# A decoder layer's down projection: all subtractions on VectorE, the operands' splits spread over five block products, two token blocks' norms without GpSimd

## The chip, the cores and the metric

One core of one Trainium2 chip runs the whole layer as one program. The metric is the device time of one execution in microseconds (us), and the time of a kernel is the median of its timed runs.

## The reference

One decoder layer on 512 tokens of width 1024, all float32: a first sublayer (sparse attention and a gated convolution, merged and projected) and a second one, the part that the change touches:

```python
gu = causal_dwconv(h @ w_ffn_up[i], ffn_conv_w[i], ffn_conv_b[i])      # 1024 -> 2 x 2816
g_ffn, u_ffn = jnp.split(gu, 2, axis=-1)
ffn = (jax.nn.silu(g_ffn) * u_ffn) @ w_ffn_down[i]                     # 2816 -> 1024
ple = jax.nn.sigmoid(h @ w_ple_gate[i] + b_ple_gate[i]) * (p[i] @ w_ple[i])
h = layer_norm(DEEPNORM_ALPHA * h + ffn + ple, ln2_g[i], ln2_b[i])     # over the 1024 columns
```

## The kernel before, in words

**Products in three parts.** Every large product is made of three matmuls. Each operand is split into a rounded copy `hi` and a rest `lo = raw - hi`, and hi·hi, hi·lo and lo·hi are summed in PSUM. A split is a copy on ScalarE (line 61 for weights, 1037 for activations; the trace calls it CAST) and then a subtraction with both inputs in SBUF. For the weights of this stage the subtraction is on VectorE (line 63), for the activations of the down projection on GpSimd (line 1038).

**Weights.** A chunk is 128x1024 (512 KB), the sixth of each product 128x512. `Chunk.dma` loads it through SP's queue into one of 4 raw buffers (`wr`), and `Chunk.split` writes `wh` and `wl`, 4 buffers each. `run` goes through a fixed list of steps. Ahead of step i, `advance` splits the chunk that step i+3 uses, and asks for the next load, which waits for the raw buffer: until VectorE has made the `wl` of four chunks before. `wh` and `wl` come free when TensorE has finished the step of four chunks before. Then the step's `preps` are issued, then the step. Engines work through their own instructions in program order.

**The down projection by seven block products.** The 2816 rows (22 groups of 128) are halved, the 1024 output columns (halves F0 and F1) too, and so are the 512 tokens: e stands for the early token blocks 0 and 1, l for the late ones 2 and 3. Seven products of half size (a Strassen scheme) take the place of eight; `PRODUCTS` names each one's weight sum, its activation operand (B11, B21, T2, T4, T3, T1, B22, in this order) and its PSUM bank. Products 0 to 5 take six steps each (11 row groups x 2 token blocks x 3 matmuls of 512 columns). The seventh (B22) takes two steps, and then one tail step for each late token block, with four chunks (38 to 41, counted from 0 at the first product). For token block 3 its columns are cut in two of 256.

**Operands.** `take_part(name, q)` splits a third of an activation operand (4, 4 and 3 groups of 128x256). Before the change the thirds of an operand are taken in steps 0, 2 and 4 of the product ahead of the one that uses it, so B22's fall into the sixth product.

**After the products.** `after_product` adds PSUM to the residual `hr` on VectorE (lines 1069, 1071) and takes statistics (1075). After the fifth product token blocks 0 and 1 are complete, and `last_norm` norms them within the sixth product (after its second and fourth step): columns F1 on VectorE by two `scalar_tensor_tensor` (lines 1139 and 1143), columns F0 by one ScalarE activation (1130) and two GpSimd operations (1131, 1132). `finish_late` adds the sixth product to blocks 2 and 3; `tail` adds the seventh, takes their last statistics and calls `last_norm` for them. Block 2 has 448 of its columns normed by GpSimd, block 3 none. Outputs of blocks 0 and 1 leave through SP's queue, in program order with the loads.

Of the kernel before, what the change touches and what calls it, by code (L numbers as in the profile page):

```python
# [8 lines left out]
F32 = mybir.dt.float32  # L9
F32R = mybir.dt.float32r  # L10
AF = mybir.ActivationFunctionType
OP = mybir.AluOpType

P = 128
S = 512
D = 1024
NB = S // P
# [20 lines left out]
class Chunk:  # L38
# [13 lines left out]
    def split(self):  # L52
        k, nc = self.k, self.k.nc
        if self.resident:
            self.hi = k.k4(f"wh{self.n}", F32R)
            self.lo = k.k4(f"wl{self.n}", F32R)
        else:
            self.hi = k.wpool.tile([P, 1024], F32R, name=f"wh{self.n}", tag="wh", bufs=k.WHL)
            self.lo = k.wpool.tile([P, 1024], F32R, name=f"wl{self.n}", tag="wl", bufs=k.WHL)
        hi, lo, raw = (t[:, self.cols] for t in (self.hi, self.lo, self.raw))  # L60
        nc.scalar.copy(hi, raw)  # L61
        eng = nc.vector if self.lo_eng == "v" else nc.gpsimd
        eng.tensor_tensor(lo, raw, hi.bitcast(F32), op=OP.subtract)  # L63


class Kern:
# [47 lines left out]

    def sm(self, name, shape, dt=F32, bufs=1):
        return self.small.tile(list(shape), dt, name=f"{name}_{self.counter()}", tag=name, bufs=bufs)

    def evac_split(self, hi, lo, src):
        self.nc.scalar.copy(hi, src)
        self.nc.vector.tensor_tensor(lo, src, hi.bitcast(F32), op=OP.subtract)  # L120
# [324 lines left out]
    def plan(self):  # L445
        nc, a = self.nc, self.a
# [5 lines left out]
        def chunk(src, **kw):  # L452
            c = Chunk(self, src, **kw)
            self.chunks.append(c)
            return c

        def step(fn, ws=()):
            i = len(self.steps)
            for w in ws:
                if w.need is None:  # L460
                    w.need = i
                w.last = i
            self.steps.append(fn)

        def wa(i, **kw):
            return chunk(a["w_a"][i], **kw)
# [286 lines left out]
        def wb(i, **kw):  # L753
            return chunk(a["w_b"][i], **kw)
# [43 lines left out]
        for i, o in enumerate(order):  # L798
            if o[0] == "g":
                w = wa(20 + 2 * o[1] + o[2], lo="p" if i <= max(att_at) else "v")  # L800
                fn = gate(o[1], o[2], w)
            elif o[0] == "r":
                w = chunk(a["w_br"][2 * o[1] + o[2]], lo="p" if i <= max(att_at) else "v")
                fn = branch(o[1], o[2], w)
            elif o[0] == "q":
                w = wa(4 + o[1], lo="v" if o[1] == 1 else "p")
                fn = qatt(o[1], w)
            else:
                w = wa(8 + 3 * o[1] + "cxb".index(o[0]), lo="p")
# [4 lines left out]
            n = att_at.get(i)  # L814
# [80 lines left out]
        for kk in range(4):  # L895
            w = wb(kk)
# [21 lines left out]
        pc, w = chunk(a["p_T"]), wb(9)  # L918
# [90 lines left out]
        for j in range(NF):  # L1009
            for which in (0, 1):  # L1010
                w = wa(36 + 2 * j + which)
                step(ffn(j, which, w), [w])
        for n, (name, i) in enumerate(copies):
# [5 lines left out]
        PRODUCTS = ((wd[0], "B11", "X"), (wd[1], "B21", "Y"), (sd["acd"], "T2", "X"), (wd[3], "T4", "W"),  # L1019
                    (sd["ac"], "T3", "X"), (sd["cd"], "T1", "Z"), (sd["abcd"], "B22", "V"))  # L1020
        self.banks, self.mv2 = {}, {}
        F0, F1 = slice(0, 512), slice(512, 1024)

        def take_part(name, q):

            n = 4 if q < 2 else HALF - 8
            if name == "B21":
                if q == 0:
                    t = [self.main.tile([P, 4, 2, S], F32R, name=f"B21{x}", tag="hT", bufs=2) for x in "hl"]
                    self.b21 = [x.rearrange("p c h (s t) -> p (c h s) t", t=256) for x in t]  # L1030
                hi, lo = (t[:, 4 * q:4 * q + 4] for t in self.b21)
            else:
                hi, lo = (self.k4(f"{name}{x}{q}", F32R, (P, 4, 256)) for x in "hl")
            for t, ts in zip((hi, lo), self.split.setdefault(name, ([], []))):
                ts.append(t)
            raw = self.part[name][q]
            nc.scalar.copy(hi[:, :n], raw[:, :n])
            nc.gpsimd.tensor_tensor(lo[:, :n], raw[:, :n], hi[:, :n].bitcast(F32), op=OP.subtract)

        def load_last():  # L1040
            self.st2 = {b: self.sm("st2", [P, 4, 6], bufs=4) for b in range(NB)}
            self.g2, self.b2 = ([self.k2(f"{n}{h}") for h in range(2)] for n in ("g2", "b2"))
            for n, ts in (("ln2_g", self.g2), ("ln2_b", self.b2)):
                v = a[n]
                for h in range(2):
                    nc.gpsimd.dma_start(ts[h], bass.AP(tensor=v.tensor, offset=v.offset + 512 * h,
                                                       ap=[[0, P], [1, 512]]))
# [18 lines left out]
        def add_to(b, fs, o, op=OP.add):  # L1066
            z = self.h1[b][:, fs]
            if op is OP.add:
                nc.vector.tensor_tensor(z, o, z, op=OP.add)  # L1069
            else:  # L1070
                nc.vector.tensor_tensor(z, z, o, op=op)

        def part_stats(b, fs):
            for i in range(fs.start // 256, fs.stop // 256):
                nc.vector.bn_stats(self.st2[b][:, i], self.h1[b][:, i * 256:i * 256 + 256])  # L1075

        def after_product(n):

            o = [x[0] for x in self.banks[PRODUCTS[n][2]]]
            for i in range(2):  # L1080
                e, l = i, 2 + i
                if n in (0, 1):
                    add_to(e, F0, o[i])
                    if n == 1:
                        part_stats(e, F0)
                elif n == 2:
                    add_to(l, F0, o[i])
                elif n == 3:
                    add_to(e, F1, o[i])
                elif n == 4:  # L1090
                    add_to(e, F1, o[i], OP.subtract)
                    part_stats(e, F1)
                    self.mv2[e] = self.ln_aggr(self.st2[e])
                    add_to(l, F1, o[i], OP.subtract)

        def finish_late(blk):

            o, b = self.banks["Z"][blk][0], 2 + blk
            add_to(b, F1, o)
            part_stats(b, F1)  # L1100
            add_to(b, F0, o, OP.subtract)

        def product(n, kk, w):
# [14 lines left out]
                    finish_late(kk)  # L1118
            return f

        def last_norm(b):
            by_pool = (512, 512, 448, 0)[b]
            z, st = self.h1[b], self.st2[b]
            rows = self.out[b * P:(b + 1) * P, :]
            gb = [[t[q.start // 512][:, q.start % 512:][:, :q.stop - q.start] for t in (self.g2, self.b2)]
                  for q in (slice(0, by_pool), F1, slice(by_pool, 512)) if q.start < 512 or q is F1]
            if by_pool:
                mv, r, nmr = self.mv2.pop(b) if b in self.mv2 else self.ln_aggr(st)
                q = slice(0, by_pool)
                nc.scalar.activation(z[:, q], z[:, q], AF.Identity, bias=nmr, scale=r)  # L1130
                nc.gpsimd.tensor_tensor(z[:, q], z[:, q], gb[0][0], op=OP.mult)
                nc.gpsimd.tensor_tensor(z[:, q], z[:, q], gb[0][1], op=OP.add)
            else:
                mv = self.sm("mv", [P, 2], bufs=4)
                nc.vector.bn_aggr(mv, st)  # L1135
                r = self.rstd(mv[:, 1:2])
            qs = list(zip([F1, slice(by_pool, 512)], gb[1:]))[:2 if by_pool < 512 else 1]
            for q, (g, _) in qs:
                nc.vector.scalar_tensor_tensor(z[:, q], z[:, q], mv[:, 0:1], g, op0=OP.subtract, op1=OP.mult)  # L1139

            def rest():
                for q, (_, be) in qs:
                    nc.vector.scalar_tensor_tensor(z[:, q], z[:, q], r, be, op0=OP.mult, op1=OP.add)  # L1143
                nc.sync.dma_start(rows[:, 512:], z[:, 512:])
                (nc.sync if b < 2 else nc.scalar).dma_start(rows[:, :512], z[:, :512])

            if b == NB - 2:
                self.pending.append(rest)
            else:
                rest()  # L1150
# [13 lines left out]
            return f  # L1164

        self.pending = []
        for n, (src, name, bank) in enumerate(PRODUCTS):
            for kk in range(NCH if n < 6 else NCH - TAILC):
                w = chunk(src[kk], cols=1024 if kk < NCH - 1 else 512)
                if n < 6 and kk % 2 == 0:  # L1170
                    nxt = PRODUCTS[n + 1][1]
                    self.preps.setdefault(len(self.steps), []).append(lambda x=nxt, q=kk // 2: take_part(x, q))
                step(product(n, kk, w), [w])
        ws = [chunk(sd["abcd"][kk], resident=kk > 3, cols=1024 if kk < NCH - 1 else 512) for kk in range(NCH - TAILC, NCH)]
        for blk in range(2):
# [2 lines left out]
        nxt = 10 ** 9  # L1178
        for c in reversed(self.chunks):
            c.due = max(min(c.need - c.lead, nxt - 1 if c.last > c.need else nxt), c.after)  # L1180
            nxt = c.due
# [124 lines left out]
```

## Time and profile before

| | us |
|---|---|
| median of 3 runs | 777.62 (777.22 to 778.82) |
| the profiled execution's own time | 781.65 |
| its span in the trace | 779.9 |
| TensorE busy, of the span | 757.8 |
| VectorE busy | 530.2 |
| ScalarE busy | 339.7 |
| GpSimd busy | 313.7 |

Times in the trace count from the span's start. The seven products run from about 659 us on. A row of the timeline gives start and duration of an instruction; on VectorE durations overlap the next instruction's start a little, so what one costs in a row of several is read from start to start. An idle time in brackets names what ended it.

### The profile page before, as it was taken

The page shows a single profiled execution, that of the slowest core. Times are in us where ns is not written, and L with a number is a line of the kernel's source. Part 1 is how long each engine was busy: PE and PEld are TensorE (multiplying, and loading weights), DVE is VectorE, ACT ScalarE, POOL GpSimd, SP SyncE. Part 2 cuts the span into 40 slices and gives each one's busy share as a digit, 9 for nine tenths or more (in the row PEclk, how much of TensorE's full clock was granted, in tenths as well). Part 3 has the DMA queues.
Part 4 walks back from the last instruction along what each step waited for, and adds up shares of the span by engine and source line. Part 5 has one row for each costly group of instructions (what it writes and reads, how often), then busy time and mean ns, then how long its engine had stood idle before and what let it go on. Part 6 is the DMA issues. An engine that isn't in the chain of part 4 may idle for free. (4 is left out here: it accounts for less than half of the span.)

```text
span 779.9 us, 9590 instructions
## 1 busy us (share of the span) xinstructions
PE 757.8 (97%) x3579; PEld 629.5 (81%) x3579; DVE 530.2 (68%) x798; ACT 339.7 (44%) x509; POOL 313.7 (40%) x230
## 2 busy tenths in 40 slices
PE   8899999999999999999999999999999999999976
PEld 5898888878878888888888888888888888888855
DVE  5878999766566349758634656566655666886797
ACT  4456334476666233242413443443343334555630
POOL 3324666643222029746211322333323332845482
PEclk9999999999999999999999999999999999999998
DMA  8372232232202156787714588777832332666551
GB/s 317 76 256 95 82 109 81 82 109 82 82 27 102 62 188 220 260 286 275 254 70 146 144 208 199 185 183 192 211 108 82 108 93 82 203 224 199 170 176 55
DMA packets 31183, 118.61 MB, mean 152 GB/s; under 512 B 3824, under 2 KB 3952, under 8 KB 30752
## 3 DMA queue, kind: packets, MB, share of 16 engines
q1 hardware_dynamic: 25536, 99.37, 36.7%
q0 software_dynamic: 4592, 16.39, 10.6%
q10 hardware_dynamic: 1008, 2.25, 0.7%
q8 instruction: 28, 0.46, 0.2%
q14 instruction: 19, 0.16, 0.1%
HBM read 112.74 MB, written 30.41 MB: 184 GB/s over the span
## 5 line engine op out<-in xcount | busy, mean ns | idle before, releaser
L63 DVE TENSOR_TENSOR wl<-wr,wh 128x1024 fp32r<-128x1024 f32 x114 | 180.9, 1604 | 104.6 <-ACT wh L61 104.6
L61 ACT CAST wh<-wr 128x1024 fp32r<-128x1024 f32 x149 | 152.1, 1027 | 77.7 <-PE dn L1064 28.1
L130 PE MATMUL ff<-h1T,wh 128*128 128x512 f32 x352 | 136.9, 389 | 0.0
L131 PE MATMUL ff<-h1T,wh 128*128 128x512 f32 x352 | 136.9, 389 | 0.0
L132 PE MATMUL ff<-h1T,wl 128*128 128x512 f32 x352 | 136.9, 389 | 0.0
L63 POOL TENSOR_TENSOR wl<-wr,wh 128x1024 fp32r<-128x1024 f32 x35 | 87.3, 2499 | 92.8 <-ACT wh L61 80.7
L130 PEld LDWEIGHTS ff<-h1T,wh 128*128 128x128 f32 x352 | 66.1, 188 | 13.8
L132 PEld LDWEIGHTS ff<-h1T,wl 128*128 128x128 f32 x352 | 66.1, 188 | 13.7
L131 PEld LDWEIGHTS ff<-h1T,wh 128*128 128x128 f32 x352 | 66.1, 188 | 13.6
L657 ACT ACTIVATE ff<-ff,vec 128x512 f32<-128x512 f32 x44 | 34.4, 781 | 79.6 <-PE ff L132 78.9
L658 DVE SCALAR_TENSOR_TENSOR ff<-ff,vec,ff 128x511 f32<-128x511 f32 x44 | 33.0, 749 | 37.1 <-ACT ff L657 37.0
L130 PE MATMUL gt<-hT,wh 128*128 128x512 f32 x128 | 50.5, 395 | 0.5 <-DVE ol L120 0.4
L132 PE MATMUL gt<-hT,wl 128*128 128x512 f32 x128 | 49.9, 390 | 0.0
L131 PE MATMUL gt<-hT,wh 128*128 128x512 f32 x128 | 49.9, 389 | 0.0
L988 POOL TENSOR_TENSOR B11l<-ff,B11h 128x256 fp32r<-128x256 f32 x11 | 8.2, 742 | 90.4 <-ACT B11h L987 90.4
L982 POOL TENSOR_TENSOR T<-T,B 128x256 f32<-128x256 f32 x11 | 9.2, 838 | 82.1 <-DVE B L978 82.1
L660 DVE SCALAR_TENSOR_TENSOR ff<-ff,vec,ff 128x510 f32<-128x510 f32 x44 | 32.9, 749 | 1.6
L130 PE MATMUL cv<-hT,wh 128*128 128x512 f32 x80 | 31.4, 392 | 0.0
L132 PE MATMUL cv<-hT,wl 128*128 128x512 f32 x80 | 31.1, 389 | 0.0
L131 PE MATMUL cv<-hT,wh 128*128 128x512 f32 x80 | 31.1, 389 | 0.0
L130 PEld LDWEIGHTS gt<-hT,wh 128*128 128x128 f32 x128 | 24.0, 188 | 6.6 <-PE lg L139 0.7
L970 ACT ACTIVATE ff<-ff 128x512 f32<-128x512 f32 x22 | 13.9, 632 | 35.0 <-DVE ff L660 35.0
(291 smaller groups left out, 1716.3 us busy)
## 6 DMA issues: line engine op xcount, KB each, us to landing
wr<-in_w_a SPq DMA_DIRECT2D x80, 512.0 KB, 3.6
wr<-in_w_b SPq DMA_DIRECT2D x17, 512.0 KB, 3.9
wr<-in_w_dn SPq DMA_DIRECT2D x15, 512.0 KB, 3.4
wr<-in_w_br SPq DMA_DIRECT2D x8, 512.0 KB, 3.3
sdac<-in_w_dn SPq DMA_DIRECT2D x6, 512.0 KB, 4.7
sdcd<-in_w_dn SPq DMA_DIRECT2D x6, 512.0 KB, 6.9
sdacd<-in_w_dn SPq DMA_DIRECT2D x6, 512.0 KB, 5.8
sdabcd<-in_w_dn SPq DMA_DIRECT2D x6, 512.0 KB, 5.5
```

The source lines that it names most:

```text
L61: nc.scalar.copy(hi, raw)
L63: eng.tensor_tensor(lo, raw, hi.bitcast(F32), op=OP.subtract)
L130: t.matmul(out, wh, xh, start=start, stop=False)
L131: t.matmul(out, wh, xl, start=False, stop=False)
L132: t.matmul(out, wl, xh, start=False, stop=stop)
L657: nc.scalar.activation(dst, src, AF.Identity, bias=v[:, bcol:bcol + 1], scale=v[:, wcol + 2 * tap:wcol + 2 * tap + 1])
L658: nc.vector.scalar_tensor_tensor(dst[:, 1:], src[:, :S - 1], v[:, wcol + tap:wcol + tap + 1], dst[:, 1:], op0=OP.mult, op1=OP.add)
L660: nc.vector.scalar_tensor_tensor(dst[:, 2:], src[:, :S - 2], v[:, wcol:wcol + 1], dst[:, 2:], op0=OP.mult, op1=OP.add)
L970: nc.scalar.activation(t, t, AF.Silu)
L982: g.tensor_tensor(p["T2"], p["T1"], second, op=OP.subtract)
L988: g.tensor_tensor(lo, first, hi.bitcast(F32), op=OP.subtract)
```

## The change

Four things change, all in the down projection.

- `take_part` puts its subtraction on VectorE. `low` is a new helper for it and for the weights' subtraction.
- The 18 thirds are no longer taken in steps 0, 2 and 4 of the product ahead, but spread over the first 30 steps (five products): number i ahead of step 8i/5. B22's last third is split ahead of step 27, not ahead of step 34. T1's split takes the two buffers that B21's has left, in place of six others.
- Token blocks 0 and 1 are normed by VectorE alone: four `scalar_tensor_tensor` each, no ScalarE activation, no GpSimd multiplication and addition. Block 2 keeps its GpSimd share.
- The statistics of blocks 0 to 2 are taken 512 columns at a time, not 256.

```diff
-        eng = nc.vector if self.lo_eng == "v" else nc.gpsimd
-        eng.tensor_tensor(lo, raw, hi.bitcast(F32), op=OP.subtract)
+        k.low(self.lo_eng, lo, raw, hi)
...
+    def low(self, eng, lo, raw, hi):
+        (self.nc.vector if eng == "v" else self.nc.gpsimd).tensor_tensor(lo, raw, hi.bitcast(F32), op=OP.subtract)
...
-            if name == "B21":
+            if name in ("B21", "T1"):
...
-            nc.gpsimd.tensor_tensor(lo[:, :n], raw[:, :n], hi[:, :n].bitcast(F32), op=OP.subtract)
+            self.low("v", lo[:, :n], raw[:, :n], hi[:, :n])
...
         def part_stats(b, fs):
-            for i in range(fs.start // 256, fs.stop // 256):
-                nc.vector.bn_stats(self.st2[b][:, i], self.h1[b][:, i * 256:i * 256 + 256])
+            w = 256 if b == NB - 1 else 512
+            for i in range(fs.start // w, fs.stop // w):
+                nc.vector.bn_stats(self.st2[b][:, i], self.h1[b][:, i * w:i * w + w])
...
-                    self.mv2[e] = self.ln_aggr(self.st2[e])
+                    self.mv2[e] = mean_rstd(self.st2[e])
...
         def last_norm(b):
-            by_pool = (512, 512, 448, 0)[b]
+            by_pool = (0, 0, 448, 0)[b]
...
-                mv = self.sm("mv", [P, 2], bufs=4)
-                nc.vector.bn_aggr(mv, st)
-                r = self.rstd(mv[:, 1:2])
-            qs = list(zip([F1, slice(by_pool, 512)], gb[1:]))[:2 if by_pool < 512 else 1]
+                mv, r = self.mv2.pop(b) if b in self.mv2 else mean_rstd(st)
+            qs = list(zip([F1, slice(by_pool, 512)], gb[1:]))
...
         self.pending = []
+        for i, (name, q) in enumerate((p[1], q) for p in PRODUCTS[1:] for q in range(3)):
+            self.preps.setdefault(len(self.steps) + 8 * i // 5, []).append(lambda x=name, q=q: take_part(x, q))
         for n, (src, name, bank) in enumerate(PRODUCTS):
             for kk in range(NCH if n < 6 else NCH - TAILC):
                 w = chunk(src[kk], cols=1024 if kk < NCH - 1 else 512)
-                if n < 6 and kk % 2 == 0:
-                    nxt = PRODUCTS[n + 1][1]
-                    self.preps.setdefault(len(self.steps), []).append(lambda x=nxt, q=kk // 2: take_part(x, q))
                 step(product(n, kk, w), [w])
```

How VectorE's instructions stand, first at the norms of token blocks 0 and 1 in the sixth product. `wl` is the rest of a weight chunk (33 to 37 here), `hr_2786` and `hr_2790` are blocks 0 and 1. Before:

```order
L63 TENSOR_TENSOR wl_6173<-wr_6074,wh_6172 128x1024
L63 TENSOR_TENSOR wl_6197<-wr_6096,wh_6196 128x1024
L1139 SCALAR_TENSOR_TENSOR hr_2786<-hr_2786,mv_6147,g_5563 128x512
L1143 SCALAR_TENSOR_TENSOR hr_2786<-hr_2786,rstd_6152,b_5565 128x512
L63 TENSOR_TENSOR wl_6222<-wr_6114,wh_6221 128x512
L63 TENSOR_TENSOR wl_6244<-wr_6136,wh_6243 128x1024
L1139 SCALAR_TENSOR_TENSOR hr_2790<-hr_2790,mv_6161,g_5563 128x512
L1143 SCALAR_TENSOR_TENSOR hr_2790<-hr_2790,rstd_6166,b_5565 128x512
L63 TENSOR_TENSOR wl_6269<-wr_6176,wh_6268 128x1024
```

Now, the same place:

```order
L118 TENSOR_TENSOR wl_6169<-wr_6084,wh_6168 128x1024
L118 TENSOR_TENSOR wl_6189<-wr_6102,wh_6188 128x1024
L1145 SCALAR_TENSOR_TENSOR hr_2786<-hr_2786,mv_6152,g_5563 128x512
L1145 SCALAR_TENSOR_TENSOR hr_2786<-hr_2786,mv_6152,g_5562 128x512
L1149 SCALAR_TENSOR_TENSOR hr_2786<-hr_2786,rstd_6156,b_5565 128x512
L1149 SCALAR_TENSOR_TENSOR hr_2786<-hr_2786,rstd_6156,b_5564 128x512
L118 TENSOR_TENSOR wl_6213<-wr_6124,wh_6212 128x512
L118 TENSOR_TENSOR wl_6231<-wr_6142,wh_6230 128x1024
L1145 SCALAR_TENSOR_TENSOR hr_2790<-hr_2790,mv_6161,g_5563 128x512
L1145 SCALAR_TENSOR_TENSOR hr_2790<-hr_2790,mv_6161,g_5562 128x512
L1149 SCALAR_TENSOR_TENSOR hr_2790<-hr_2790,rstd_6165,b_5565 128x512
L1149 SCALAR_TENSOR_TENSOR hr_2790<-hr_2790,rstd_6165,b_5564 128x512
```

Each norm is two instructions longer on VectorE, and the weights' rests behind it (chunks 35 and 36, then 37) stand behind four of them, not two.

VectorE at the start of the first product, now:

```order
L118 TENSOR_TENSOR wl_5549<-wr_5400,wh_5548 128x1024
L118 TENSOR_TENSOR B21l<-B_4771,B21h 128x1024
L118 TENSOR_TENSOR wl_5585<-wr_5436,wh_5584 128x1024
L118 TENSOR_TENSOR B21l<-B_5081,B21h 128x1024
L118 TENSOR_TENSOR wl_5605<-wr_5476,wh_5604 128x512
L118 TENSOR_TENSOR wl_5623<-wr_5512,wh_5622 128x1024
L118 TENSOR_TENSOR B21l<-B_5389,B21h 128x768
```

The operands' rests stand between the weights' rests; before the change the four `wl` stood here one behind the other, and the `B21l` on GpSimd.

GpSimd in the sixth product, before, between the two `rstd` and block 2's:

```order
L1038 TENSOR_TENSOR B22l_6179<-B_4772,B22h_6178 128x1024
L1131 TENSOR_TENSOR hr_2786<-hr_2786,g_5562 128x512
L1132 TENSOR_TENSOR hr_2786<-hr_2786,b_5564 128x512
L1038 TENSOR_TENSOR B22l_6228<-B_5082,B22h_6227 128x1024
L1131 TENSOR_TENSOR hr_2790<-hr_2790,g_5562 128x512
L1132 TENSOR_TENSOR hr_2790<-hr_2790,b_5564 128x512
L1038 TENSOR_TENSOR B22l_6275<-B_5390,B22h_6274 128x768
```

None of these seven is left on GpSimd; what it keeps there are the `rstd` of one element in each partition.

## Rows read from the trace of the kernel before

**Rows 1.** The page: busy time of each engine, its share of the span and instructions; and TensorE's granted clock in 40 slices of the span, in tenths of full speed.

```profile
PE 757.8 (97%) x3579; PEld 629.5 (81%) x3579; DVE 530.2 (68%) x798; ACT 339.7 (44%) x509; POOL 313.7 (40%) x230
PEclk9999999999999999999999999999999999999998
```

**Rows 2.** Stretches of the span: length, busy us of each engine (instructions), granted clock, DMA share, GB/s.

```profile
661.00:733.70 72.70, 72.47 (x319) 59.35 (x318) 56.68 (x44) 40.54 (x43) 43.69 (x22) 1.00 0.61 204
...
740.00:760.00 20.00, 14.43 (x64) 11.20 (x63) 19.80 (x11) 7.61 (x8) 16.67 (x8) 0.96 0.52 170
...
758.00:760.00 2.00, 2.00 (x6) 1.58 (x7) 2.00 (x2) 0.00 (x0) 0.00 (x0) 0.60 0.42 119
760.00:762.00 2.00, 2.00 (x12) 2.00 (x11) 2.00 (x4) 0.62 (x1) 0.00 (x0) 0.54 0.03 12
```

**Rows 3.** Timeline of TensorE in the down projection: start us, us, engine, line, operation, out<-in, shapes; in brackets idle time before it and what ended it.

```profile
679.10 0.50 PE L1063 MATMUL dn<-wl,B21h 128*128 128x512 f32 x1 [0.23 <-DVE wl L63]
...
718.73 0.39 PE L1062 MATMUL dn<-wh,T3h 128*128 128x512 f32 x1
...
733.69 0.39 PE L1062 MATMUL dn<-wh,T1h 128*128 128x512 f32 x1
...
748.51 0.50 PE L1063 MATMUL dn<-wl,T1h 128*128 128x512 f32 x1 [0.84 <-DVE wl L63]
...
751.84 0.50 PE L1063 MATMUL dn<-wl,B22h 128*128 128x512 f32 x1 [1.67 <-DVE wl L63]
...
757.98 0.50 PE L1063 MATMUL dn<-wl,B22h 128*128 128x512 f32 x1 [3.06 <-DVE wl L63]
...
761.85 0.28 PE L1062 MATMUL dn<-wh,B22h 128*128 128x256 f32 x1
761.97 0.28 PE L1063 MATMUL dn<-wl,B22h 128*128 128x256 f32 x1
...
766.75 0.39 PE L1064 MATMUL dn<-wh,B22l 128*128 128x512 f32 x1
```

**Rows 4.** Timeline of VectorE (DVE) from the end of the fifth product to its last rows, same columns; like neighbours are one row (x2: two instructions).

```profile
734.84 0.68 DVE L1071 TENSOR_TENSOR hr<-hr,dn 128x512 f32<-128x512 f32 x1
735.55 0.75 DVE L1075 BATCH_NORM_STATS2 st<-hr 128x6 f32<-128x256 f32 x2
736.34 0.26 DVE L168 BATCH_NORM_AGGREGATE mv<-st 128x2 f32<-128x24 f32 x1
...
739.88 2.36 DVE L63 TENSOR_TENSOR wl<-wr,wh 128x1024 fp32r<-128x1024 f32 x2
742.15 2.91 DVE L1139 SCALAR_TENSOR_TENSOR hr<-hr,mv,g 128x512 f32<-128x512 f32 x1
745.15 1.61 DVE L1143 SCALAR_TENSOR_TENSOR hr<-hr,rstd,b 128x512 f32<-128x512 f32 x1
746.69 5.10 DVE L63 TENSOR_TENSOR wl<-wr,wh 128x512 fp32r<-128x512 f32 x2
751.71 1.77 DVE L1139 SCALAR_TENSOR_TENSOR hr<-hr,mv,g 128x512 f32<-128x512 f32 x1
753.59 1.60 DVE L1143 SCALAR_TENSOR_TENSOR hr<-hr,rstd,b 128x512 f32<-128x512 f32 x1
755.11 6.83 DVE L63 TENSOR_TENSOR wl<-wr,wh 128x1024 fp32r<-128x1024 f32 x5
761.86 0.68 DVE L1069 TENSOR_TENSOR hr<-dn,hr 128x512 f32<-128x512 f32 x1
...
765.22 0.67 DVE L1071 TENSOR_TENSOR hr<-hr,dn 128x512 f32<-128x512 f32 x1
767.18 0.69 DVE L1069 TENSOR_TENSOR hr<-dn,hr 128x512 f32<-128x512 f32 x1 [1.29 <-PE dn L1064]
...
773.84 1.41 DVE L1139 SCALAR_TENSOR_TENSOR hr<-hr,mv,g 128x512 f32<-128x512 f32 x2
775.16 1.41 DVE L1143 SCALAR_TENSOR_TENSOR hr<-hr,rstd,b 128x512 f32<-128x512 f32 x2
```

**Rows 5.** Timeline of GpSimd (POOL) in the sixth product and behind it, same columns.

```profile
741.11 3.40 POOL L1038 TENSOR_TENSOR B22l<-B,B22h 128x1024 fp32r<-128x1024 f32 x1
...
747.87 2.83 POOL L1038 TENSOR_TENSOR B22l<-B,B22h 128x1024 fp32r<-128x1024 f32 x1
...
754.59 2.25 POOL L1038 TENSOR_TENSOR B22l<-B,B22h 128x768 fp32r<-128x768 f32 x1
```

**Rows 6.** Timelines of VectorE and of GpSimd in the first product and at the start of the second, same columns.

```profile
661.33 4.59 DVE L63 TENSOR_TENSOR wl<-wr,wh 128x1024 fp32r<-128x1024 f32 x3
...
670.24 5.47 DVE L63 TENSOR_TENSOR wl<-wr,wh 128x1024 fp32r<-128x1024 f32 x1 [0.97 <-ACT wh L61]
...
675.63 3.42 DVE L63 TENSOR_TENSOR wl<-wr,wh 128x1024 fp32r<-128x1024 f32 x1
...
670.39 4.22 POOL L1038 TENSOR_TENSOR B21l<-B,B21h 128x1024 fp32r<-128x1024 f32 x2
```

**Rows 7.** VectorE's line 63 from 640 us on (durations ns min/median/max); VectorE's statistics of 512 columns in the first sublayer, by line (busy us, mean ns); and the time from issue to landing of the weight loads from 640 us on.

```profile
L63 DVE TENSOR_TENSOR wl<-wr,wh x43: 677/1226/5471, 639.6 to 761.3; 128x1024 fp32r<-128x1024 f32 x36, 128x512 fp32r<-128x512 f32 x7
...
L161 DVE BATCH_NORM_STATS2 st<-hr 128x6 f32<-128x512 f32 x8 | 5.6, 695 | 0.3
...
DMA to landing us min/median/max: 2.5/3.4/6.3
```

More of the change, by code (lines that the diff above doesn't have):

```diff
@@ L1026, in take_part @@
             n = 4 if q < 2 else HALF - 8
-            if name == "B21":
+            if name in ("B21", "T1"):
                 if q == 0:
-                    t = [self.main.tile([P, 4, 2, S], F32R, name=f"B21{x}", tag="hT", bufs=2) for x in "hl"]
-                    self.b21 = [x.rearrange("p c h (s t) -> p (c h s) t", t=256) for x in t]
-                hi, lo = (t[:, 4 * q:4 * q + 4] for t in self.b21)
+                    t = [self.main.tile([P, 4, 2, S], F32R, name=f"{name}{x}", tag="hT", bufs=2) for x in "hl"]
+                    self.in_hT = [x.rearrange("p c h (s t) -> p (c h s) t", t=256) for x in t]
+                hi, lo = (t[:, 4 * q:4 * q + 4] for t in self.in_hT)
             else:
@@ L1037, in take_part @@
             nc.scalar.copy(hi[:, :n], raw[:, :n])
-            nc.gpsimd.tensor_tensor(lo[:, :n], raw[:, :n], hi[:, :n].bitcast(F32), op=OP.subtract)
+            self.low("v", lo[:, :n], raw[:, :n], hi[:, :n])
         def load_last():
-            self.st2 = {b: self.sm("st2", [P, 4, 6], bufs=4) for b in range(NB)}
+            self.st2 = {b: self.sm("st2", [P, 4, 6], bufs=4)[:, :4 if b == NB - 1 else 2] for b in range(NB)}
             self.g2, self.b2 = ([self.k2(f"{n}{h}") for h in range(2)] for n in ("g2", "b2"))
@@ L1119, in product, with mean_rstd @@
             return f
+        def mean_rstd(st):
+            mv = self.sm("mv", [P, 2], bufs=4)
+            nc.vector.bn_aggr(mv, st)
+            return mv, self.rstd(mv[:, 1:2])
         def last_norm(b):
-            by_pool = (512, 512, 448, 0)[b]
+            by_pool = (0, 0, 448, 0)[b]
             z, st = self.h1[b], self.st2[b]
@@ L1125, in last_norm @@
             gb = [[t[q.start // 512][:, q.start % 512:][:, :q.stop - q.start] for t in (self.g2, self.b2)]
-                  for q in (slice(0, by_pool), F1, slice(by_pool, 512)) if q.start < 512 or q is F1]
+                  for q in (slice(0, by_pool), F1, slice(by_pool, 512))]
             if by_pool:
-                mv, r, nmr = self.mv2.pop(b) if b in self.mv2 else self.ln_aggr(st)
+                mv, r, nmr = self.ln_aggr(st)
                 q = slice(0, by_pool)
```

## The prediction

> **What bounds the kernel now.** I read the page first, then the stretches, then the timelines of the last 45 us. The page says TensorE: 757.8 of 779.9 us busy, at a granted clock of full speed in all slices but the last [rows 1]. The stretches say the same of the first five products (72.47 of 72.70 us busy): what other engines do there costs nothing as long as TensorE isn't kept waiting. They say something else from 740 to 760: TensorE 14.43 of 20 us, VectorE 19.80, GpSimd 16.67 [rows 2]. There VectorE is what TensorE waits for. TensorE's timeline shows three stalls, of 0.84, 1.67 and 3.06 us, each ended by a `wl` of line 63; before them there is one of 0.23 us in the second product [rows 3]. [...]
>
> VectorE is full there because its instructions are long. The median `wl` takes 1.226 us, and the two at 739.88 cost 2.27 from start to start, 1.14 each; but the two at 746.69, one of them of 512 columns only, take 5.10 together. The norms' instructions take 2.91, 1.61, 1.77 and 1.60, where two of the same shape cost 1.32 and two 1.41 at the end of the kernel [rows 4, 7]. The long ones lie between 741.11 and 756.84, the start of GpSimd's first and the end of its last subtraction for B22 [rows 5]. The clearest pair is earlier: a `wl` from 670.24 takes 5.47, and GpSimd works from 670.39 for 4.22; 4.22 + 1.23 is 5.45 [rows 6]. I take from this that the long times are waits for GpSimd, which ends with GpSimd's work.
>
> **Part 1: 18 splits on VectorE, in five products.** A product takes 733.69 - 718.73 = 14.96 us of TensorE, five take 74.8 [rows 3]. VectorE's work in them: 25 `wl` of 1024 at 1.14 and 5 of 512 at 0.60 (0.677 less the same overlap of 0.08), 31.5 us [rows 4, 7]. The new ones are the same operation on the same types: 12 of 1024 at 1.14, 6 of 768 at 0.87 (halfway between), 18.9. VectorE has no such split in the trace, so the lower bound is that, the upper GpSimd's own 2.11 (4.22 for two, of 1024 and 768) [rows 6]. I take the lower, since engine, operation, size and types agree. The adds and statistics behind four products are some 3 x 1.3 + 2.8 = 6.7, eight adds and four statistics at about 0.65 and 0.75 (as the rows at 734.84 and 735.55 space them) [rows 4]. That makes 57 of 74.8 us: it fits, and TensorE covers it. A `wl` is asked for three steps (8.2 us) before its use, and the lag of before, 4.2 us at 670.24 and 2.2 at 675.63, cost TensorE 0.23 us in all [rows 3, 6]. So the splits cost nothing here, and the 0.23 goes. By the upper price VectorE would need 76 us (18 x 2.11 = 38.0 in place of 18.9), 1.4 more than there is: 770.8 in the end. ScalarE's copies only move, with 40.54 of 72.70 us used [rows 2].
>
> **Part 2: what stands behind the fifth product.** The first add starts at 734.84, now 0.23 earlier: 734.61. From it to the next `wl` it is 5.04 us now. Two pairs of statistics at 0.79 each (735.55 to 736.34) become two single ones of 0.70 + 0.04; two small instructions of one element go. I take 4.85, and `wl` 33 starts at 739.46 [rows 4, 7].
>
> **Part 3: the norms and the weights' rests.** Chunks 33 and 34 take 2.27: 741.73. Norm of block 0: four at 0.70 (1.32 and 1.41 for two), 2.80: 744.53. Chunks 35 and 36, 0.60 + 1.14: 746.27. Norm of block 1: 749.07. Chunk 37: 750.21. Chunks 38 to 40 and 41, 3.42 + 0.60: 754.23. The additions of the sixth product to blocks 2 and 3 took 761.86 to 765.89, less 0.06: VectorE is free at 758.20 [rows 4]. The price of the four is the unsure term: 0.70 alone, 1.97 as the mean of the four long ones. I take 0.70, since nothing long is left on GpSimd to meet them.
>
> [...] By the rows the path gets shorter, since the work handed out stretches what stays.
>
> TensorE then needs `wl` 35 at 747.29, 36 at 748.65, both less 0.23, 37 after a step of 6 x 0.227 + 12 x 0.12 = 2.80 more, at 751.45. They are there at 745.1, 746.3 and 750.2 (0.227 is 14.96/66, 0.12 is 761.97 - 761.85) [rows 3]. [...]
>
> **Part 4: the end.** TensorE starts the seventh product at 748.42, ends its two steps at 754.02 and block 2's 21 matmuls (4.76) at 758.78. The last of them starts at 758.56, and the add of VectorE starts 0.43 after it, as 767.18 does after 766.75: **758.99** [rows 3, 4]. VectorE has been free since 758.20, 0.79 us of slack. From here on, as before, VectorE works without a gap to the end (9.4 us) and two stores follow; that part keeps its length.
>
> **Sum.** 767.18 - 758.99 = 8.2 us. Against the profiled execution: 781.65 - 8.2 = 773.4. That one stands 4.03 us above the median of the runs; from the median it is 777.62 - 8.2 = **769.4 us**. A difference of 0.2% (1.6 us) is about what a measurement here can tell from none.
>
> **Loads.** Chunk 41's load waits for `wl` 37 and stands behind block 1's two stores on SP. Issued at 750.3 with the median of 3.4 us it is there at 753.7, its copy 0.6 later, just as VectorE comes to it. With the longest landing, 6.3 [rows 7], it is there at 756.6, copied at 757.2, its `wl` done at 757.9, and VectorE is free at 761.9: a gain of 5.3.
>
> **Rivals.**
> 1. *The last load is late* (above): 772.3 us. For it: the stores of 256 KB each go out just before. Against: the median, and a chunk of half size. Chance 0.10.
> 2. *A lag in the first product.* GpSimd still ends its last sums there and issues four loads of gains and biases, and VectorE now has three more subtractions in the same steps. Three `wl` beside GpSimd took 1.53 each [rows 6]; five instead of three cost 0.8 us more lag, and a repeat of 4.2 + 2.2 on top makes 7.2 of the 8.2 us at hand. If it overruns, it is by 1 to 2 us, as part 1's upper price would: 771. Chance 0.06.
> 3. *VectorE is full by its own work* (the other side). If the long times come from something that stays (operands, the transfers beside them), the four added instructions cost between 2.8 and 4 x 1.97 = 7.9 on the path: 780.4 to 785.5. It decides where the eight average above 0.70 + (767.18 - 758.20)/8 = 1.82 us. Against it: every long one overlaps GpSimd, and short ones of the same shape lie beside them. Chance 0.05.
> 4. *No change*: only the `wl` get short, and the norms stay at 1.7 to 1.9 each, near rival 3's turning point: 776.6 to 778.2, since VectorE is then free at 766.2 to 767.8. The mean of the four long ones allows it, the two prices at the kernel's end don't. Chance 0.03.
>
> **How the numbers follow.** The forecast has 0.76; its own range is 768.2 (run to run some 0.4 below, and a little more from the end) to 771.0 (1.2 above for run to run, and norms of 0.9 each, which eat the slack of 0.79 and 0.8 more). With rivals 1 and 2 the range is 768.2 to 773.0; outside it lie rivals 3 and 4 and the edges, 0.13. Faster: 0.76 + 0.10 + 0.06 = 0.92; same 0.03; slower 0.05.
>
> **What would show it.** Right: no stall of TensorE between 733 and 759 over 0.3 us, clock at full speed there; `wl` of 1024 at 1.2 us throughout, norms at 0.7; the splits at 1.2 on VectorE, with GpSimd nearly idle; the first add behind block 2's tail at 759 and the span at 771.7. Wrong: long norms or `wl` with GpSimd idle (rival 3), ScalarE waiting for the last load at 754 to 757 (rival 1), or stalls by `wl` in the first five products (rival 2).

## The result, and the profile after

The changed kernel takes **770.38 us** (median of 4 runs, 770.31 to 770.46) against 778.22 us of the kernel before beside it: a ratio of 0.9893, 95% interval 0.9865 to 0.9921. The forecast was 769.4 us with a range of 768.2 to 773.0; by the two medians the gain is 7.8 us, forecast were 8.2.

One thing has to be known to compare traces. Executions differ in when the first block product begins, mostly by 2.6 to 3 us and in one trace by 6, and what makes the difference lies more than 500 us ahead of anything the change touches (see "The start"). In the profiled execution of the kernel before it began late, in that of the changed kernel early. These are the first matmuls of the first product in the two timelines of TensorE, before and after:

```profile
658.07 0.39 PE L1062 MATMUL dn<-wh,B11h 128*128 128x512 f32 x1
```

```profile
655.09 0.39 PE L1064 MATMUL dn<-wh,B11h 128*128 128x512 f32 x1
```

So I measure a *section*: from this matmul to the start of the last pair of norm instructions on VectorE, 775.16 before [rows 4] and 763.53 below. It is 117.09 us before and 108.44 after, a gain of **8.65 us**. The spans, 779.9 and 768.5, differ by 11.4: the section, 2.98 of the start, less 0.2 by which the changed kernel takes longer behind the section. A section is of one execution. The one of the kernel before took 781.65 us; with an early start it would take some 778.7 (an estimate, less 2.98). The lowest run of that kernel is 777.22, of the changed one 770.31, a gain of 6.9; where the former saves another 1.5 us no trace shows.

The changed kernel's stretches (columns as in [rows 2]): TensorE is busy throughout and at full clock, where it had 14.43 of 20 us and, for 4 us, granted clocks of 0.60 and 0.54.

```profile
661.00:733.40 72.40, 72.40 (x321) 59.99 (x320) 58.98 (x63) 42.24 (x46) 4.11 (x6) 1.00 0.64 213
740.00:760.00 20.00, 20.00 (x120) 17.81 (x119) 18.36 (x31) 5.60 (x6) 1.45 (x3) 1.00 0.41 141
```

VectorE's timeline, for [rows 4]; L118 is the subtraction of weights and of operands, L1145 and L1149 are the norms:

```profile
730.96 0.68 DVE L1073 TENSOR_TENSOR hr<-hr,dn 128x512 f32<-128x512 f32 x1
...
735.66 2.35 DVE L118 TENSOR_TENSOR wl<-wr,wh 128x1024 fp32r<-128x1024 f32 x2
737.93 1.41 DVE L1145 SCALAR_TENSOR_TENSOR hr<-hr,mv,g 128x512 f32<-128x512 f32 x2
739.26 1.41 DVE L1149 SCALAR_TENSOR_TENSOR hr<-hr,rstd,b 128x512 f32<-128x512 f32 x2
740.58 1.82 DVE L118 TENSOR_TENSOR wl<-wr,wh 128x512 fp32r<-128x512 f32 x2
...
744.97 2.36 DVE L118 TENSOR_TENSOR wl<-wr,wh 128x1024 fp32r<-128x1024 f32 x2
748.49 2.41 DVE L118 TENSOR_TENSOR wl<-wr,wh 128x1024 fp32r<-128x1024 f32 x2 [1.16 <-ACT wh L61]
751.17 0.69 DVE L118 TENSOR_TENSOR wl<-wr,wh 128x512 fp32r<-128x512 f32 x1 [0.27 <-ACT wh L61]
751.78 0.69 DVE L1071 TENSOR_TENSOR hr<-dn,hr 128x512 f32<-128x512 f32 x1
...
755.67 0.69 DVE L1071 TENSOR_TENSOR hr<-dn,hr 128x512 f32<-128x512 f32 x1
...
763.53 1.41 DVE L1149 SCALAR_TENSOR_TENSOR hr<-hr,rstd,b 128x512 f32<-128x512 f32 x2
```

Nothing is long any more at the norms: four norm instructions cost 2.65 us, 737.93 to 740.58, where two took 4.5 (742.15 to 746.69). VectorE waits twice, for copies of weights on ScalarE (1.16 and 0.27). The row at 755.67 is the add behind block 2's tail, 767.18 before. It doesn't wait for TensorE: the last matmul that it needs started at 755.02, and at the 0.43 us that lay between the two before it could have started at 755.45.

```profile
755.02 0.39 PE L1066 MATMUL dn<-wh,B22l 128*128 128x512 f32 x1
```

Why the copies were late, from ScalarE's timeline and the landing of the loads of `sdabcd` in the changed kernel:

```profile
747.41 2.24 ACT L61 CAST wh<-wr 128x1024 fp32r<-128x1024 f32 x2 [2.66 <-DVE wl L118]
750.51 0.62 ACT L61 CAST wh<-wr 128x512 fp32r<-128x512 f32 x1 [0.87 <-DMA wr<-sdabcd]
...
DMA to landing us min/median/max: 3.3/4.2/6.1
```

The first wait is put down to a `wl`, but the `wl` that could hold that buffer, chunk 35's, had ended at 741.3. The load issued then, at 741.4, takes 5.9 us to land and is there at 747.4; the next one takes the longest, 6.1. Both ran beside block 0's two stores, issued at 740.03 and 740.69. The median of these six loads is 4.2 us; for the same six it was 3.3 in the kernel before (2.6 to 4.5).

### The profile page after: what moved, and what is told of

Read it like the earlier page. It is cut to its first block, busy times and chain, and to the rows that moved or that the text cites. A ratio compares the mean times of both kernels' runs of the same rounds, so it can differ in the third digit from the quotient of the medians.

```text
span 768.5 us, 9566 instructions
## 1 busy us (share of the span) xinstructions
PE 752.3 (98%) x3579; PEld 626.2 (81%) x3579; DVE 521.2 (68%) x812; ACT 338.1 (44%) x507; POOL 260.5 (34%) x206
## 5 line engine op out<-in xcount | busy, mean ns | idle before, releaser
L118 DVE TENSOR_TENSOR wl<-wr,wh 128x1024 fp32r<-128x1024 f32 x114 | 158.5, 1400 | 104.2 <-ACT wh L61 104.1
L118 POOL TENSOR_TENSOR wl<-wr,wh 128x1024 fp32r<-128x1024 f32 x35 | 88.1, 2520 | 93.9 <-ACT wh L61 91.0
L659 ACT ACTIVATE ff<-ff,vec 128x512 f32<-128x512 f32 x44 | 34.4, 781 | 79.5 <-PE ff L134 78.7
L150 POOL TENSOR_TENSOR rstd<-veps,neghalf 128x1 f32<-128x1 f32 x12 | 11.6, 966 | 107.0 <-DVE veps L148 79.4
```

The costliest lines, as they stand in the source:

```text
L118: (self.nc.vector if eng == "v" else self.nc.gpsimd).tensor_tensor(lo, raw, hi.bitcast(F32), op=OP.subtract)
L150: nc.gpsimd.tensor_tensor(r, v, self.neghalf, op=OP.pow)
L659: nc.scalar.activation(dst, src, AF.Identity, bias=v[:, bcol:bcol + 1], scale=v[:, wcol + 2 * tap:wcol + 2 * tap + 1])
```

## The experiments

The two parts that could make the gain are *who* subtracts for the operands (GpSimd or VectorE) and *where* (old steps, or spread over five products); the norms are a third. Four kernels vary them; the statistics of 512 columns and T1's buffers stay as changed in all four.

| splits on | splits where | norms 0, 1 by | section us | median us | ratio to before (95%) |
|---|---|---|---|---|---|
| GpSimd | old steps | GpSimd (kernel before) | 117.09 | 778.22 | 1 |
| GpSimd | old steps | VectorE | 114.35 | 776.75 | 0.9985 (0.9958 to 1.0013) |
| GpSimd | spread | VectorE | 114.81 | 777.53 | 0.9994 (0.9977 to 1.0011) |
| VectorE | old steps | VectorE | 109.90 | 771.84 | 0.9923 (0.9895 to 0.9952) |
| VectorE | spread | GpSimd | 109.96 | 771.41 | 0.9915 (0.9883 to 0.9947) |
| VectorE | spread | VectorE (the change) | 108.44 | 770.38 | 0.9893 (0.9865 to 0.9921) |

By the times, the second and third kernel of the table can't be told from the kernel before: both intervals hold 1. That the norms' move alone gains, 2.74 us by the sections of one execution each, is thus not shown by the times.

### Splits back on GpSimd, still spread

```diff
-            self.low("v", lo[:, :n], raw[:, :n], hi[:, :n])
+            self.low("p", lo[:, :n], raw[:, :n], hi[:, :n])
```

> The changed kernel (770.4 us), with the 18 operand splits back on GpSimd but in their new, spread places (none in the sixth product); norms of blocks 0 and 1 stay on VectorE. Theory (the long VectorE times are waits for GpSimd, and only those in the sixth product and behind it reach TensorE): the end is the same as in the changed kernel; in the five products some wl take 2.5 to 5 us again, at a cost of 0 to 1.4 us: 770.4 to 771.8 us. Rival (VectorE is simply the quicker engine for the splits, wherever they stand): 18 splits x 1.2 us more each, part of it seen by TensorE: 774 us or more.

Measured: 777.53 us. My theory's time fell. Its end did hold: from the third product's first matmul to the last norms the section is as long as in the changed kernel (78.7 and 78.5 us). All of the loss, 6.2 us, is in the second product. TensorE, VectorE and GpSimd there:

```profile
677.54 0.73 PE L1065 MATMUL dn<-wl,B21h 128*128 128x512 f32 x1 [4.24 <-DVE wl L118]
```

```profile
667.39 10.09 DVE L118 TENSOR_TENSOR wl<-wr,wh 128x1024 fp32r<-128x1024 f32 x1 [0.97 <-ACT wh L61]
```

```profile
667.57 4.21 POOL L118 TENSOR_TENSOR B21l<-B,B21h 128x1024 fp32r<-128x1024 f32 x2
671.73 4.67 POOL L118 TENSOR_TENSOR T2l<-T,T2h 128x1024 fp32r<-128x1024 f32 x2
```

One `wl` waited for four GpSimd subtractions in a row: 0.18 + 4.16 + 4.67 + 1.1 of its own is 10.1. TensorE stood for 4.24 us, and the clock was granted at 0.50 for 2 us afterwards:

```profile
678.00:680.00 2.00, 2.00 (x6) 1.54 (x5) 2.00 (x4) 0.00 (x0) 0.00 (x0) 0.50 0.53 143
```

Bringing the splits forward alone, on GpSimd, is thus worth nothing (114.81 against 114.35): what it gains at the end it loses where GpSimd's work gets denser.

### The same, thinner

Is it the pile-up in the second product, or GpSimd beside VectorE anywhere? The same kernel, with other steps:

```diff
-            self.preps.setdefault(len(self.steps) + 8 * i // 5, []).append(lambda x=name, q=q: take_part(x, q))
+            self.preps.setdefault(len(self.steps) + (2 * i if i < 7 else 12 + 15 * (i - 6) // 11), []).append(lambda x=name, q=q: take_part(x, q))
```

> The changed kernel with the 18 splits on GpSimd, as in the run that lost 6.3 us in the second product, but spaced so that they don't stand back to back there: i = 0 to 6 ahead of steps 0, 2, ... 12, the other eleven evenly over steps 13 to 27; none in the sixth product. Theory (that run's loss is a pile-up: four GpSimd subtractions in a row locked one wl out for 10.1 us): the longest wl is 5 to 6 us as in the kernel before, the second product loses 0.8 us or less, and the rest is as in the changed kernel: 771.2 to 772.5 us. Rival (18 subtractions on GpSimd beside VectorE cost that much wherever they stand): 775 us or more.

Measured: 773.51 us, ratio 0.9902 (0.9867 to 0.9936), section 112.82: between the two. The second product lost 0.8 us as expected, but the fourth and fifth took 16.35 and 16.40 us from first matmul to first matmul, where 14.96 is the usual, so they lost 1.4 each, and three thirds of T4 and three of T3 were subtracted back to back, though they are split ahead of different steps:

```profile
690.05 16.86 DVE L118 TENSOR_TENSOR wl<-wr,wh 128x1024 fp32r<-128x1024 f32 x6
```

```profile
690.38 8.75 POOL L118 TENSOR_TENSOR T4l<-T,T4h 128x1024 fp32r<-128x1024 f32 x3 [3.98 <-ACT T4h L1039]
699.09 9.53 POOL L118 TENSOR_TENSOR T3l<-T,T3h 128x1024 fp32r<-128x1024 f32 x3
```

The likely reading, not tested by itself: a VectorE that falls behind delays the steps, and GpSimd's work bunches up. So both the theory (772.5 at most) and the rival (775 at least) were off.

### Splits on VectorE, in their old steps

```diff
-            self.preps.setdefault(len(self.steps) + 8 * i // 5, []).append(lambda x=name, q=q: take_part(x, q))
+            self.preps.setdefault(len(self.steps) + 2 * i, []).append(lambda x=name, q=q: take_part(x, q))
```

> The changed kernel, all splits on VectorE, but in their old steps (0, 2 and 4 of the product ahead), so that B22's three fall into the sixth product. Theory: nothing is long there, but VectorE's own chain gets 1.14 + 1.14 + 0.87 = 3.15 us longer, wl 37 and with it the last load come 3.15 later: the first add behind block 2's tail 3.2 later, TensorE stalls about 0.8 us by wl 37: 773.6 us (773.0 to 774.0). Rival (the place doesn't matter, only the engine): 770.4 us.

Measured: 771.84 us, 1.46 us more than the changed kernel both by the section and by the medians; 3.2 were expected, none by the rival. VectorE at the place:

```profile
749.30 4.09 DVE L118 TENSOR_TENSOR wl<-wr,wh 128x1024 fp32r<-128x1024 f32 x4
753.30 0.68 DVE L1071 TENSOR_TENSOR hr<-dn,hr 128x512 f32<-128x512 f32 x1
```

The chain is 3.15 us longer, but the four last `wl` run without the waits of 1.16 and 0.27: the three added subtractions fill time that VectorE would have waited for loads. The add behind block 2's tail comes 1.5 later (757.19).

### Norms back on GpSimd, and norms alone

```diff
-            by_pool = (0, 0, 448, 0)[b]
+            by_pool = (512, 512, 448, 0)[b]
...
```

> The changed kernel, but columns F0 of blocks 0 and 1 normed by ScalarE and GpSimd as before (512 columns each: one activation, two GpSimd operations); splits on VectorE and spread. Theory: VectorE loses four instructions (2.65 us) but waits for four GpSimd operations of about 1.3 us each alone (448 columns take 1.13 to 1.14 at the kernel's end): between 0 and 5.2 us of waits, so 769.9 (the floor that TensorE sets) to 773 us, likeliest 771.5. Rival (more work on a full VectorE only lengthens its chain, and GpSimd costs it nothing): 770.1 us, at the floor, and no long VectorE instruction.

Measured: 771.41 us, as the theory's likeliest. VectorE and GpSimd:

```profile
737.86 1.78 DVE L1145 SCALAR_TENSOR_TENSOR hr<-hr,mv,g 128x512 f32<-128x512 f32 x1
739.74 1.61 DVE L1149 SCALAR_TENSOR_TENSOR hr<-hr,rstd,b 128x512 f32<-128x512 f32 x1
741.27 4.01 DVE L118 TENSOR_TENSOR wl<-wr,wh 128x512 fp32r<-128x512 f32 x2
```

```profile
736.81 2.29 POOL L1139 TENSOR_TENSOR hr<-hr,g 128x512 f32<-128x512 f32 x1
```

With two instructions a norm in place of four, VectorE is later: its `wl` 37 starts 91.8 us behind the first matmul, where it is 89.9 in the changed kernel. Handing the work out cost more in waits here than it saved: the section is 109.96 us, not 108.44. The fourth kernel has splits on GpSimd in the old steps, and only the norms moved (`"p"` and `2 * i`, as in the diffs above).

> The kernel before with the norms of blocks 0 and 1 on VectorE alone (and statistics of 512 columns, T1's split in B21's buffers): splits on GpSimd in their old steps. Theory: GpSimd's three splits for B22 (2.4, 2.4 and 2.1 us alone) still stand beside VectorE's chain there, which has 2.8 us more to do than in the kernel before but four GpSimd operations fewer to wait for: up to 6.9 us of waits over the changed kernel, 773 to 777.3 us, likeliest 775. Rival (the norms' move makes all of the gain): 770.4 us. Rival (the norms' move is a loss by itself, of 2.8 us on a full engine): 781 us.

Measured: 776.75 us, within the theory's range and 1.75 above its likeliest. The splits for B22 stand beside the chain, and two `wl` take 4.56, two norm instructions 5.12, beside two GpSimd subtractions stretched to 6.74:

```profile
742.51 4.56 DVE L118 TENSOR_TENSOR wl<-wr,wh 128x1024 fp32r<-128x1024 f32 x2
746.99 5.12 DVE L1145 SCALAR_TENSOR_TENSOR hr<-hr,mv,g 128x512 f32<-128x512 f32 x2
```

```profile
742.60 6.74 POOL L118 TENSOR_TENSOR B22l<-B,B22h 128x1024 fp32r<-128x1024 f32 x2
```

### GpSimd work that reads, and work that only writes

The direct test of the cause: the changed kernel, with GpSimd work added that nothing waits for. Both are put behind block 0's norm in program order.

```diff
+                if n == 5 and kk == 1:
+                    x = self.k2("extra")
+                    for _ in range(9):
+                        nc.gpsimd.tensor_tensor(x, self.g2[0], self.b2[0], op=OP.add)
```

> The changed kernel with nine more GpSimd operations on 128x512 in the sixth product, behind the rstd of block 1 (g2 + b2 into a spare tile that nobody reads): about 1.27 us each alone, 11.4 us in all, with no dependence on VectorE's work. Theory (VectorE's instructions with two SBUF inputs wait while GpSimd reads SBUF): wl and norms from 736 on get long again, TensorE stalls by wl, 774 to 780 us. Rival (the long times had another cause): 770.4 us.

```diff
...
+                    for _ in range(22):
+                        nc.gpsimd.memset(x, 0.0)
```

> The same place, but 22 GpSimd memsets of 128x512 into the spare tile (0.52 us each alone by the first memset of that size in the trace, 11.4 us in all): GpSimd writes SBUF and reads none. Theory A (it is GpSimd's reading that VectorE waits for): nothing gets long, 770.4 us. Theory B (any GpSimd work beside it blocks VectorE): as with the reads, 774 to 780 us.

Measured: 779.2 us with the reads (ratio 0.9984, 0.9962 to 1.0007: the gain can't be seen any more), 770.06 with the writes (two runs; 0.986, 0.9816 to 0.9904). The sections are 116.30 and 108.30 us, 108.44 without either. VectorE and GpSimd with the reads:

```profile
739.12 3.48 DVE L1149 SCALAR_TENSOR_TENSOR hr<-hr,mv,g 128x512 f32<-128x512 f32 x2
742.52 3.45 DVE L1153 SCALAR_TENSOR_TENSOR hr<-hr,rstd,b 128x512 f32<-128x512 f32 x2
```

```profile
735.83 16.86 POOL L1123 TENSOR_TENSOR extra<-g,b 128x512 f32<-128x512 f32 x9
```

and with the writes:

```profile
738.35 1.41 DVE L1149 SCALAR_TENSOR_TENSOR hr<-hr,mv,g 128x512 f32<-128x512 f32 x2
739.67 1.40 DVE L1153 SCALAR_TENSOR_TENSOR hr<-hr,rstd,b 128x512 f32<-128x512 f32 x2
```

```profile
736.14 12.79 POOL L1123 MEMSET extra<- 128x512 f32 x22
```

The same norm instructions cost 1.7 us each beside a GpSimd that reads and 0.66 beside one that is just as busy writing. What goes with the long times is thus GpSimd's reading, not its being busy (3.48 and 1.41 us for two). A wait could be longer than one GpSimd instruction: the `wl` of 10.09 us in the kernel with the splits back on GpSimd waited for four.

### Stores later, block 2 on VectorE, both, and the change again

What is left in the last 20 us. Stores of blocks 0 and 1 behind the last load (they are kept in a list and issued in the seventh product's two steps):

```diff
+                if b < 2:
+                    self.stores.append(store)
+                else:
+                    store()
...
                 if n == 6:
                     finish_late(kk)
+                    self.stores.pop(0)()
```

> The changed kernel with the stores of blocks 0 and 1 issued behind the last weight load on SP (in the two steps of the seventh product). Theory (VectorE waited 1.16 and 0.27 us for copies of weights whose loads ran beside these stores; TensorE's last matmul of block 2's tail sets the floor, 0.22 us below): those waits go, the first add behind block 2's tail comes 0.2 us earlier, 770.2 us against 770.4: not to be told from none by the time, by the trace yes. Rival (loads take 4.2 us for another reason): the waits stay, 770.4.

Block 2's norm on VectorE:

```diff
-            by_pool = (0, 0, 448, 0)[b]
+            by_pool = (0, 0, 0, 0)[b]
```

> The changed kernel with block 2's norm on VectorE alone too (0 of 448 columns on GpSimd): VectorE gains some 0.9 us of own work (448 columns in two instructions) and loses the wait at 759.15, where two instructions of 512 and 64 columns take 1.86 beside GpSimd. Theory: within 0.3 us of the changed kernel, 770.1 to 770.7. Rival (GpSimd's share is worth its 2.3 us there): 772 or more.

> Stores later and block 2's norm on VectorE alone, together. If the two are independent: 769.9 to 770.5 us; a version that beats the changed kernel would show 769.6 or less.

> The changed kernel itself, beside the three others: 770.4 us (770.2 to 770.6).

Measured: medians 770.16, 771.61, 770.19 and 770.53 us; lowest runs 770.08, 770.07, 769.91 and 770.30. The 771.61 lies between early and late starts (three of its six runs at 770.07 to 770.33, three at 772.89 to 773.22), so again the sections: 108.22, 108.17, 108.16, and 108.47 for the change again. All three gain 0.25 to 0.3 us, and not more together. With the stores later VectorE runs ahead and waits for TensorE (this kernel's start was late, so its times stand 2.7 us higher):

```profile
747.66 4.62 DVE L118 TENSOR_TENSOR wl<-wr,wh 128x1024 fp32r<-128x1024 f32 x4
752.46 0.69 DVE L118 TENSOR_TENSOR wl<-wr,wh 128x512 fp32r<-128x512 f32 x1 [0.17 <-ACT wh L61]
...
758.14 0.69 DVE L1071 TENSOR_TENSOR hr<-dn,hr 128x512 f32<-128x512 f32 x1 [1.10 <-PE dn L1066]
```

The wait of 1.16 is gone, 1.10 of slack stands behind block 2's tail, and TensorE sets the time. In the kernel with block 2 alone on VectorE the waits were smaller too (0.66 in one place, with the stores where they were), and VectorE waited 0.60 for TensorE there. So its 0.3 us is not shown to come from the norm: loads that landed sooner (4.8 us at most, not 6.1) would do. That GpSimd's share of 448 columns is worth nothing here is shown. By the times none of the four can be told from another.

### The start

> Stores later and block 2's norm on VectorE, and at the kernel's start GpSimd's three small loads (kv_norm_g, k_idx_ln_g, k_idx_ln_b) issued ahead of its first wl, not behind it. Theory (the spread of the runs of one kernel, 770.3 against 772.8, comes from the start: where GpSimd's first wl starts at 19.4 to 19.7 us, just ahead of VectorE's second hT subtraction, that subtraction waits for it, 4.5 us for the two in place of 2.35, and the first product begins 2.6 us later; where it starts at 20.0 or later it does not): GpSimd's wl always starts after 20, every execution has the early start, the first product begins at 655.0, and all runs lie at 769.8 to 770.4 us with none at 772 to 773. Rival (the two levels have another cause): about one run in three at 772.5 to 773.

```diff
         wx_split(3, nc.gpsimd)
+        self.bcast("kv_norm_g", R, self.kvg)
+        self.bcast("k_idx_ln_g", 64, self.kig)
+        self.bcast("k_idx_ln_b", 64, self.kib)
```

(and the three lines are taken away where they stood.) The kernel also has the stores later and block 2's norm on VectorE. What led to it, VectorE and GpSimd at the start of the kernel before and, behind it, of the changed one:

```profile
18.64 4.51 DVE L278 TENSOR_TENSOR hT<-hx,hT 128x1024 fp32r<-128x1024 f32 x2
19.65 2.43 POOL L63 TENSOR_TENSOR wl<-wr,wh 128x1024 fp32r<-128x1024 f32 x1 [1.48 <-ACT wh L61]
```

```profile
18.62 2.35 DVE L280 TENSOR_TENSOR hT<-hx,hT 128x1024 fp32r<-128x1024 f32 x2
20.10 3.14 POOL L118 TENSOR_TENSOR wl<-wr,wh 128x1024 fp32r<-128x1024 f32 x1 [2.23 <-ACT wh L61]
```

In the first GpSimd starts at 19.65, and VectorE's second subtraction waits for it: 4.51 us for the pair, where it is 2.35 with GpSimd's start at 20.10. Of the 14 traces three have the pair at 4.5 us, and these three begin the first product at 657.7 to 658.1; ten have it at 2.35 and begin at 654.9 to 655.5. Measured: 770.04 us, ratio 0.9895 (0.9877 to 0.9912), five of six runs at 769.86 to 770.26 and one at 772.81; section 108.17. The theory said none at 772 to 773, so it doesn't explain all late starts, or GpSimd's subtraction can still come first; this late run has no trace, and that stays open. But the fourteenth trace shows a second cause. In the kernel with the norms alone moved, the `hT` pair took 2.35 us, and the first product still began at 661.04. One VectorE instruction, with a single SBUF input, took 7.29 us there and 1.30 in the changed kernel:

```profile
94.58 7.29 DVE L535 TENSOR_SCALAR madd<-tk 128x256 f32<-128x256 f32 x1
```

```profile
94.63 1.30 DVE L535 TENSOR_SCALAR madd<-tk 128x256 f32<-128x256 f32 x1
```

GpSimd went through the same operations in both, one behind the other, up to 101.7. In the first VectorE came through only behind the last of them, in the second behind the one that ran when it began:

```profile
99.30 2.42 POOL L118 TENSOR_TENSOR wl<-wr,wh 128x1024 fp32r<-128x1024 f32 x1
```

The 6.0 us are the whole lateness of that trace (661.04 against 655.09). By its median the kernel of this section is the best version tried, but not by more than a measurement here can tell.

## Why the prediction was right

**What bounds the kernel** (VectorE between 740 and 760, by waits for GpSimd): right, and shown by the reads and the writes, not only by times that overlap. One reading was too strong: a 9 of the page's clock row means 90% or more, not full speed, and the clock of 0.96 from 740 to 760 [rows 2] lies under a 9.

**Part 1, the splits.** Price right: 1.13 us from start to start for an operand's 1024 (1.14 forecast), 1.22 in duration, as a `wl`:

```profile
718.33 1.22 DVE L118 TENSOR_TENSOR B22l<-B,B22h 128x1024 fp32r<-128x1024 f32 x1
719.46 1.22 DVE L118 TENSOR_TENSOR wl<-wr,wh 128x1024 fp32r<-128x1024 f32 x1
```

TensorE covers them, 72.40 of 72.40 us. Mis-sized was what goes away: not the 0.23 us of the one stall that the timeline of the matmuls named, but 0.8. The second product took 15.8 us before, 15.0 after, first matmul to first matmul; the `wl` was late for the load of the weights into TensorE (PEld) too, twice in the kernel before and never in the changed one:

```profile
679.10 0.19 PEld L1063 LDWEIGHTS dn<-wl,B21h 128*128 128x128 f32 x1 [0.66 <-DVE wl L63]
...
684.78 0.19 PEld L1063 LDWEIGHTS dn<-wl,B21h 128*128 128x128 f32 x1 [0.37 <-DVE wl L63]
```

And I read the old places (GpSimd costs the five products next to nothing) as if it held for any places, in what I expected of the first experiment. The two kernels with GpSimd's splits spread lost 6.2 and 3.6 us in these products. What each move is worth alone I had not seen: by the sections the other engine gains 4.45 us in the old steps already, while the spread costs 0.46 us on GpSimd and gains 1.46 on VectorE.

**Parts 2 and 3, the chain.** 4.70 us behind the fifth product (4.85 forecast), 2.65 for a norm (2.80), 1.14 for a `wl`. Not forecast were the waits of 1.16 and 0.27 for copies. I had checked the last load only, at the median landing and, in rival 1, at the longest; the wait for chunk 39, loaded beside block 0's stores, was the longer.

**Part 4, the floor.** The step that failed is the slack: VectorE was to be free 0.79 us ahead of TensorE and was 0.22 behind it. Rival 1's mechanism came, then, in a small size; with the stores moved, the wait of 1.16 is gone and that of 0.27 is 0.17.

**Sum.** Of the 8.65 us, 8.53 lie ahead of the add behind block 2's tail: 8.19 forecast, + 0.57 in the second product, - 0.22 for the late loads, 8.54. The other 0.1 is one statistics instruction in place of two, and a shorter aggregation, in the tail. That the forecast came within 1.0 us of the measured time has some luck in it: two terms missed in opposite directions, and 8.2 us, counted on an execution of 781.65, were taken off a median of 777.62.

**Rival 2** (a lag in the first product): three subtractions there took 1.75 to 1.77 us beside GpSimd's last sums, as its condition said, and TensorE lost nothing.

```profile
660.04 1.75 DVE L118 TENSOR_TENSOR B21l<-B,B21h 128x1024 fp32r<-128x1024 f32 x1
```

**Rivals 3 and 4** (VectorE full by its own work, norms staying long) are out: with 22 more instructions on VectorE (18 splits, four of the norms), none from the first product on is long without GpSimd reading: the longest subtraction took 1.77 us, beside GpSimd's last sums, and 1.23 at most behind them; a norm's instruction of blocks 0 and 1 cost 0.66. Handing a part of the norms out of the full VectorE gains nothing here, as the kernel with the norms back on GpSimd shows: 771.41, not less than 770.38.

## What to carry to other kernels

Ahead of giving work with SBUF inputs to GpSimd, look at what VectorE does at that time: here, beside nine additions on GpSimd, VectorE's norm instructions, with two SBUF inputs each, cost 1.7 us in place of 0.66, and the additions took 16.86 us in place of an estimated 11.4. Whether the number of inputs decides was not tested; the `madd` of 7.29 us has one. The row to look for is an instruction of usual shape and several times its usual length that ends about one own duration after GpSimd's (the `wl` of 5.47 us [rows 6], and that of 10.09). Where a stall of the bounding engine hangs on such a row, take GpSimd's reads out of the stretch or put them on VectorE, and count the other engine's whole run back to back (four subtractions for the 10.09 us), not one instruction, as the wait at worst. When executions differ at the start, compare sections of the traces beside the medians, and keep in mind that a section is of one execution.

## What the runs showed that I had not expected

A run of GpSimd's subtractions kept one VectorE instruction waiting for all of it: 5.47 us for two in a row [rows 6], 10.09 for four. Elsewhere both engines got longer side by side: nine additions on GpSimd stretched from 11.4 us, the estimate from 448 columns, to 16.86, while VectorE's norm instructions took 1.7 each. Which of the two happens was not settled; the `madd` of 7.29 and of 1.30 us shows both outcomes with the same instructions around it. Writes without a gap (22 memsets in 12.79 us) cost VectorE nothing that can be seen: 0.66 us for a norm's instruction, and a section of 108.30 us beside 108.44.
